# SBUF pools opened in another order, with pads, so that every float32r matmul operand starts at a multiple of 256 bytes

## The chip, the core and the metric

The kernel runs on one core of one Trainium2 chip. The metric is device time in microseconds (us) of one execution, the median of several runs. Engines are named as in the profile: PE (TensorE matmul), PEld (TensorE weight load), DVE (VectorE), ACT (ScalarE), POOL (GpSimd) and SP (SyncE, which issues the DMAs).

## The reference

A two-layer decoder trunk over 512 tokens of width 1024. Each layer is a half-step SwiGLU FFN, a token mixer and a second half-step FFN, each behind an RMS norm; a last norm ends it.

```python
def _swiglu(h, wg, wu, wd):                    # D_FF = 2816
    return (jax.nn.silu(h @ wg) * (h @ wu)) @ wd
...
    for i in range(DEPTH):                     # DEPTH = 2
        h = _rmsnorm(x, ffn1_norm[i])
        x = x + 0.5 * _swiglu(h, ffn1_w_gate[i], ffn1_w_up[i], ffn1_w_down[i])
        h = _rmsnorm(x, mix_norm[i])
        x = x + _mixing(h, positions, w_in[i], w_out[i], ...)
        h = _rmsnorm(x, ffn2_norm[i])
        x = x + 0.5 * _swiglu(h, ffn2_w_gate[i], ffn2_w_up[i], ffn2_w_down[i])
    return _rmsnorm(x, final_norm)
```

`_mixing` projects h through one matrix and runs three causal mixers on parts of the result: forgetting attention (4 heads of 64), dilated window attention (4 heads of 64, with rotary positions) and a gated linear recurrence (HGRN2, 4 heads of 128); their outputs go through one output matrix.

## The kernel before

The token dimension (512) lies along the free axis, the features in blocks of 128 on the partitions. Every large product is computed from two float32r halves of each operand: `load_split` loads a weight tile of up to 128x1024 float32 (`raw`, 3 buffers, a DMA on SP), ACT rounds it to float32r (`wh`, L243) and DVE takes the rest (`wl`, L245). Activations are split in the same way: `xh`, `xl` from x, `hh`, `hl` for the hidden layer, `oh..`, `ol..` for the mixers' outputs. `mm3` (L250 to L252) then issues three matmuls of 128x128 by 128x512 into the same PSUM tile:

```python
        PE.matmul(ps, lh, rh, start=first, stop=False)
        PE.matmul(ps, lh, rl, start=False, stop=False)
        PE.matmul(ps, ll, rh, start=False, stop=last)
```

The first operand is stationary (weights, loaded by PEld), the second is moving. Gate and up (tile `gu_ps`): 22 hidden blocks x 2 x 8 x 3 matmuls in each of 4 FFNs, weights from `wh`/`wl`, moving `xh`/`xl`. Down (`d_ps`): 8 x 22 x 3 in each FFN, moving `hh`/`hl`. The mixer's projections (`hf`, `hq`, `hi`, `dqk`, `v`, `hg`, `ff`, `fq`, `fk`) use `wh`/`wl` with `xh`/`xl` in either role (L425 to L427 are mm3 with the activations stationary). The output product (`o_ps`) has `oh`/`ol` moving. The matmuls within the mixers (`lv`, `ho`, `sc`, `po`, transposes) are plain float32.

A tile framework orders the instructions: it schedules the traced program for each engine by dependences and priorities (`high_priority(CHAIN)` for the mixers' chains), so projections fill PE between the chain's steps. Tiles with the same tag share a buffer, and a new user of a buffer waits for the old one.

SBUF tiles are placed one after another in the order in which pools are opened and their tiles are first made. In the built program the first pool begins 128 bytes past a multiple of 256. Tiles made by `lines` (statistics, scalars) are rounded up to 64 bytes; all others here but some tables are multiples of 256 bytes. Before, `const` comes first and starts with a 48-float `pad` (192 bytes); its tiles are 26 x 256 bytes in all. So `x`, `xh`, `xl`, `raw`, `wh`, `wl` begin 64 bytes past a multiple of 256. `small` shifts what follows by 128: `hh`, `hl`, and `oh`/`ol` in the mixer's pool, begin 192 bytes past. A 128-column slice is 512 bytes, so all slices used as operands keep these offsets.

In `states` (L680 to L688) four blocks b of two heads go through one PSUM tile (`ho_ps`, one buffer): up to four matmuls of a head, then DVE writes `ho` (L681), then ACT squares it into a scratch tile `hsq` and accumulates the sum in `hss` (L685). In `dilated`, DVE applies the rotary positions to `qk` through scratch tiles `ca` and `sa` (L592 to L598) before PE transposes it (`dt_ps`, L602). `hsq` and `ca` have 512 bytes and one buffer each.

Of the kernel before, what the change touches and what calls it, by code (L numbers as in the profile page):

```python
# [10 lines left out]
F32 = mybir.dt.float32  # L11
# [7 lines left out]
NB, KB, FB = T // 128, D // 128, FF // 128  # L19
# [6 lines left out]
LEVELS = (1, 2, 4, 8, 16, 32, 64)  # L26
AHEAD = 400
CHAIN = 100
PAD = 48


def shape_constants():
# [95 lines left out]
def hybrid_trunk(ctx: ExitStack, tc: tile.TileContext, a, out):  # L128
    nc = tc.nc
    V, S, G, PE = nc.vector, nc.scalar, nc.gpsimd, nc.tensor  # L130

    const = ctx.enter_context(tc.tile_pool(name="const", bufs=1))
    keep = ctx.enter_context(tc.tile_pool(name="keep", bufs=1))
    wp = ctx.enter_context(tc.tile_pool(name="wp", bufs=2))
    small = ctx.enter_context(tc.tile_pool(name="small", bufs=2))
    acc_p = ctx.enter_context(tc.tile_pool(name="acc", bufs=4, space=bass.MemoryType.PSUM))
    gen_p = ctx.enter_context(tc.tile_pool(name="gen", bufs=1, space=bass.MemoryType.PSUM))

    def lines(pool, shape, dt=F32, **kw):

        n = int(np.prod(shape[1:]))
        flat = pool.tile([shape[0], -(-n // 16) * 16], dt, **kw)[:, 0:n]
        if len(shape) == 2:
            return flat
        return flat.rearrange("p (a b) -> p a b", a=shape[1])
# [4 lines left out]
    def gen(tag, name):  # L150
        return gen_p.tile([128, 512], F32, tag=tag, name=name)


    const.tile([128, PAD], F32, name="pad")
    x = [keep.tile([128, T], F32, name=f"x{k}") for k in range(KB)]
    par = const.tile([128, 64], F32, name="par")
    raws = []
# [38 lines left out]
    def rsqrt(m, shape, tag):  # L196

        y = lines(small, shape, tag=tag + "y", name="rs_y")
        S.activation(y, m, AF.Sqrt)
        V.reciprocal(y, y)  # L200
        t = lines(small, shape, tag=tag + "t", name="rs_t")
        V.tensor_tensor(out=t, in0=y, in1=y, op=ALU.mult)
        V.tensor_tensor(out=t, in0=t, in1=m, op=ALU.mult)
        V.tensor_scalar(out=t, in0=t, scalar1=-0.5, scalar2=1.5, op0=ALU.mult, op1=ALU.add)
        r = lines(small, shape, tag=tag + "r", name="rs_r")
        V.tensor_tensor(out=r, in0=y, in1=t, op=ALU.mult)
        return r
# [190 lines left out]
    def mixing(l, after, r, rb):  # L398
# [7 lines left out]
        mp = ctx2.enter_context(tc.tile_pool(name="mix", bufs=1, reuse_waits="tile"))  # L406
# [23 lines left out]
        def slot(tag, shape, name, dt=F32, bufs=1):  # L430
            return mp.tile(list(shape), dt, tag=tag, name=name, bufs=bufs)
# [5 lines left out]
        otl = {kind: [pair(f"ol{kind}", f"ol{kind}", R32)] for kind in "fd"}  # L437
        amat, obl = {}, {}
        at = [lines(mp, [128, 8], tag=f"ad{p}", name=f"ad{p}") for p in range(2)]

        def put_out(kind, b, o, n):

            ps = gen("pt", "ot_ps")
            for i in range(n):
                PE.transpose(ps[:, i * 128:(i + 1) * 128], o[:, i * 128:(i + 1) * 128], ident)
            s = slice(b * 128, (b + 1) * 128)
            for i in range(n // 2):
                pv = ps[:, i * 256:(i + 1) * 256].rearrange("p (n t) -> p n t", n=2)
                hi, lo = oth[kind][i][:, :, s], otl[kind][i][:, :, s]
                S.copy(hi, pv)  # L450
                V.tensor_tensor(out=lo, in0=pv, in1=hi.bitcast(F32), op=ALU.subtract)
# [206 lines left out]
            return hv  # L658

        ho = [slot(f"ho{b}", (128, 4, 128), f"ho{b}") for b in range(NB)]  # L660
        hss = [lines(mp, [128, NB, 2], tag=f"hss{p}", name=f"hss{p}") for p in range(2)]
        hrs = [None, None]

        def states(p, hv):
            am, ob = amat[p], obl[p]
            for b in range(NB):
                po = gen("lv", "ho_ps")
                for hh in range(2):
                    cross = {
                        (0, 1): ob[:, 2, hh * 256:hh * 256 + 128],  # L670
                        (2, 3): ob[:, 2, hh * 256 + 128:hh * 256 + 256],
                        (0, 2): ob[:, hh, 0:128], (0, 3): ob[:, hh, 128:256],
                        (1, 2): ob[:, hh, 256:384], (1, 3): ob[:, hh, 384:512],
                    }
                    h = 2 * p + hh
                    hs = slice(h * 128, (h + 1) * 128)
                    ps = po[:, hh * 128:(hh + 1) * 128]
                    for j in range(b + 1):
                        lhs = cross[j, b] if j < b else am[:, hh, b * 128:(b + 1) * 128]
                        PE.matmul(ps, lhs, hv[j // 2][:, j % 2, hs], start=j == 0, stop=j == b)  # L680
                    V.scalar_tensor_tensor(out=ho[b][:, h, :], in0=hv[b // 2][:, b % 2, hs],  # L681
                                           scalar=at[p][:, hh * NB + b:hh * NB + b + 1], in1=ps,
                                           op0=ALU.mult, op1=ALU.add)
                    sq = mp.tile([128, 128], F32, tag="hsq", name="hsq", bufs=1)
                    S.activation(sq, ho[b][:, h, :], AF.Square, accum_out=hss[p][:, b, hh:hh + 1])  # L685
                yield
            ss = hss[p]
            V.tensor_scalar(out=ss, in0=ss, scalar1=1.0 / 128, scalar2=EPS, op0=ALU.mult, op1=ALU.add)  # L688
            hrs[p] = rsqrt(ss.rearrange("p b h -> p (b h)"), [128, 8], f"hr{p}")
# [20 lines left out]
        hv = values()  # L710
        run(d0)
        run(states(0, hv))
        run(decays(1, *decay_inputs(1)))
        run(states(1, hv))
        run(dilated())
        gated()
# [24 lines left out]
    for l in range(L):  # L741
        nrm = {}
        ffn(l, a["ffn1_w_gate"], a["ffn1_w_up"], a["ffn1_w_down"],
            lambda d: norm_block(d, gvec(("mix_norm", l), d), nrm), rb, None if l else tables)
        r, rb = norm_finish(nrm)
        nrm = {}
        with ExitStack() as ctx2:
            mixing(l, lambda d: norm_block(d, gvec(("ffn2_norm", l), d), nrm), r, rb)
        r, rb = norm_finish(nrm)
        nrm = {}  # L750
        if l + 1 < L:
            ffn(l, a["ffn2_w_gate"], a["ffn2_w_up"], a["ffn2_w_down"],
                lambda d: norm_block(d, gvec(("ffn1_norm", l + 1), d), nrm), rb)
            r, rb = norm_finish(nrm)
        else:
            def last(d):
                square_block(d, nrm)
                if d == KB - 2:
                    warm = lines(small, [128, 1], tag="warm", name="warm")
                    S.activation(warm, nrm["ss"][:, 0:1], AF.Sqrt)  # L760

            ffn(l, a["ffn2_w_gate"], a["ffn2_w_up"], a["ffn2_w_down"], last, rb)
            _, rb = norm_finish(nrm, copy=False)
            for d in range(KB):
                V.scalar_tensor_tensor(out=x[d], in0=x[d], scalar=gvec("final", d), in1=rb,
                                       op0=ALU.mult, op1=ALU.mult)
                (nc.scalar if d % 2 else nc.sync).dma_start(out=out[d * 128:(d + 1) * 128, :], in_=x[d])
# [17 lines left out]
```

## Time and profile before

| | |
|---|---|
| median of 3 runs | 2109.24 us (2109.0 to 2109.46) |
| profiled execution, its own time | 2108.85 us |
| its span, first to last instruction | 2107.1 us |
| mean granted TensorE clock | 0.997 |
| PE busy | 2080.3 us, 99% |
| DVE / ACT busy | 993.5 us (47%) / 691.6 us (33%) |
| DMA | 184.35 MB, mean 87 GB/s |

Matmuls overlap in the pipeline: a matmul's duration in the profile includes its drain, and its end is modelled. What a stream of matmuls costs is the distance from one start to the next.

### The profile page before, as it was taken

To read this page: it belongs to the slowest core of one execution; us is meant where nothing else is said; L and a number is where in the kernel's file an instruction comes from. 1 tells how busy PE (TensorE), PEld (TensorE's weight loads), DVE (VectorE), ACT (ScalarE), POOL (GpSimd) and SP (SyncE) were. 2 spreads that over 40 slices of the span, in tenths; PEclk is the share of its full clock that TensorE was granted. 3 is DMA by queue.
4 is the path that set the end of the run, shared out by engine and by line. 5 is a ranking of instruction groups with operands and counts; after the bars stand their busy time and mean duration, and the time that the engine had idled before them with its cause. 6 is when DMAs were issued, how large, how long until landed. Compare 5 with 4: busy or idle time off the path is not lost.

```text
span 2107.1 us, 23700 instructions
## 1 busy us (share of the span) xinstructions
PE 2080.3 (99%) x9622; PEld 1688.9 (80%) x9622; DVE 993.5 (47%) x1590; ACT 691.6 (33%) x1005; POOL 13.0 (1%) x18
## 2 busy tenths in 40 slices
PE   8999999999999999999999999999999999999997
PEld 6888888888777888888888888888887778888885
DVE  7444433556364544443344443336554554444323
ACT  5323222333353423222233322232344443323221
POOL 0000000000000000000000000000000000000000
PEclk9999999999999999999999999999999999999998
DMA  5322333211122222233332223332211122222332
GB/s 166 100 91 99 95 93 94 94 60 51 50 69 67 97 92 99 100 94 92 95 98 93 100 96 91 99 100 70 65 57 51 56 85 90 100 98 92 95 96 69
DMA packets 54373, 184.35 MB, mean 87 GB/s; under 512 B 6888, under 2 KB 7016, under 8 KB 54264
## 3 DMA queue, kind: packets, MB, share of 16 engines
q1 hardware_dynamic: 53656, 181.73, 27.1%
q8 instruction: 75, 1.23, 0.2%
q10 hardware_dynamic: 576, 1.05, 0.1%
q14 instruction: 34, 0.28, 0.0%
q0 software_dynamic: 32, 0.07, 0.0%
HBM read 180.69 MB, written 2.10 MB: 87 GB/s over the span
## 4 chain that ended last, share of the span: by engine, by line
PE 97%; DVE 2%; ACT 1%; DMA 0%; issue 0%; SPq 0%; DVEq 0%
PE gu_ps L252 15%; PE gu_ps L251 15%; PE gu_ps L250 15%; PE d_ps L252 8%; PE d_ps L250 8%; PE d_ps L251 8%; PE lv_ps L501 2%; PE sc_ps L552 2%; PE po L571 2%; PE o_ps L250 1%; PE o_ps L251 1%; PE o_ps L252 1%; PE ho_ps L680 1%; PE pt_ps L564 1%; PE v_ps L425 1%; PE v_ps L426 1%
## 5 line engine op out<-in xcount | busy, mean ns | idle before, releaser
L243 ACT CAST wh<-raw 128x1024 fp32r<-128x1024 f32 (+2 forms) x350 | 357.6, 1022 | 1112.7 <-issue 417.4
L245 DVE TENSOR_TENSOR wl<-raw,wh 128x1024 fp32r<-128x1024 f32 (+2 forms) x350 | 415.5, 1187 | 321.5 <-ACT wh L243 319.4
L250 PE MATMUL gu_ps<-xh,wh 128*128 128x512 f32 x1408 | 548.8, 390 | 7.5 <-ACT wh L243 7.5
L252 PE MATMUL gu_ps<-xh,wl 128*128 128x512 f32 x1408 | 550.4, 391 | 0.0
L251 PE MATMUL gu_ps<-xl,wh 128*128 128x512 f32 x1408 | 548.3, 390 | 0.0
L250 PEld LDWEIGHTS gu_ps<-xh,wh 128*128 128x128 f32 x1408 | 264.9, 188 | 63.6 <-ACT wh L243 7.5
L252 PEld LDWEIGHTS gu_ps<-xh,wl 128*128 128x128 f32 x1408 | 264.8, 188 | 56.1 <-issue 1.0
L251 PEld LDWEIGHTS gu_ps<-xl,wh 128*128 128x128 f32 x1408 | 264.8, 188 | 55.4 <-DVE xl L184 0.2
L252 PE MATMUL d_ps<-hh,wl 128*128 128x512 f32 x704 | 278.1, 395 | 0.0
L250 PE MATMUL d_ps<-hh,wh 128*128 128x512 f32 x704 | 278.1, 395 | 0.0
L251 PE MATMUL d_ps<-hl,wh 128*128 128x512 f32 x704 | 278.1, 395 | 0.0
L380 DVE TENSOR_TENSOR u<-gu_ps,rb 128x512 f32<-128x512 f32 x88 | 60.8, 691 | 269.2 <-PE gu_ps L252 269.0
L252 PEld LDWEIGHTS d_ps<-hh,wl 128*128 128x128 f32 x704 | 132.1, 188 | 32.2
L251 PEld LDWEIGHTS d_ps<-hl,wh 128*128 128x128 f32 x704 | 132.1, 188 | 32.1
L250 PEld LDWEIGHTS d_ps<-hh,wh 128*128 128x128 f32 x704 | 132.1, 188 | 32.1
L377 DVE TENSOR_TENSOR g<-gu_ps,rb 128x512 f32<-128x512 f32 x88 | 60.8, 691 | 178.7 <-PE gu_ps L252 176.6
L383 ACT CAST hh<-u 128x512 fp32r<-128x512 f32 x88 | 54.8, 623 | 61.2 <-DVE u L381 61.2
L394 DVE SCALAR_TENSOR_TENSOR x<-d_ps,x 128x512 f32<-128x512 f32 x32 | 22.1, 692 | 95.3 <-PE d_ps L252 95.3
L381 DVE TENSOR_TENSOR u<-u,g 128x512 f32<-128x512 f32 x88 | 60.9, 692 | 8.4
L501 PEld LDWEIGHTS lv_ps<-hQ,hk 128*128 128x128 f32 x448 | 55.8, 191 | 8.7 <-issue 5.9
L385 DVE TENSOR_TENSOR hl<-u,hh 128x512 fp32r<-128x512 f32 x88 | 60.3, 686 | 4.1 <-ACT hh L383 4.1
L571 PEld LDWEIGHTS po<-vv,pt 128*128 128x128 f32 x320 | 42.2, 190 | 19.7 <-DVE pt L569 7.8
(236 smaller groups left out, 2104.8 us busy)
## 6 DMA issues: line engine op xcount, KB each, us to landing
raw<-in_ffn_w_gate SPq DMA_DIRECT2D x88, 512.0 KB, 3.5
raw<-in_ffn_w_up SPq DMA_DIRECT2D x88, 512.0 KB, 3.5
raw<-in_w_in SPq DMA_DIRECT2D x58, 512.0 KB, 3.5
raw<-in_ffn_w_down SPq DMA_DIRECT2D x64, 448.0 KB, 3.3
raw<-in_ffn_w_down SPq DMA_DIRECT2D x32, 512.0 KB, 3.5
raw<-in_w_out_dh SPq DMA_DIRECT2D x16, 384.0 KB, 2.9
x<-in_x SPq DMA_DIRECT2D x8, 256.0 KB, 6.3
raw<-in_w_out_f SPq DMA_DIRECT2D x4, 512.0 KB, 3.6
```

Of the source, the lines that this page charges most:

```text
L243: S.copy(wh, raw)
L245: V.tensor_tensor(out=wl, in0=raw, in1=wh.bitcast(F32), op=ALU.subtract)
L250: PE.matmul(ps, lh, rh, start=first, stop=False)
L251: PE.matmul(ps, lh, rl, start=False, stop=False)
L252: PE.matmul(ps, ll, rh, start=False, stop=last)
L377: V.tensor_tensor(out=g, in0=part[0], in1=rb, op=ALU.mult)
L380: V.tensor_tensor(out=u, in0=part[1], in1=rb, op=ALU.mult)
L381: V.tensor_tensor(out=u, in0=u, in1=g, op=ALU.mult)
L383: S.copy(h1, u)
L385: V.tensor_tensor(out=h2, in0=u, in1=h1.bitcast(F32), op=ALU.subtract)
L501: PE.matmul(ps[:, e:e + 64], K[:, hh, s], Q[:, hh, s].rearrange("p (n two c) -> p n two c", two=2, c=c)[:, :, 1, :], start=True, stop=True)
L571: PE.matmul(po[:, h * HD:(h + 1) * HD], pt[:, j * 128:(j + 1) * 128], val[:, j, h * HD:(h + 1) * HD], start=j == 0, stop=j == b)
```

## The change

The `const` pool is opened after `keep` and `wp`; a 32-float tile (128 bytes) in a new first pool and a 96-float tile (384 bytes) in a new pool behind `small` are pads that nothing reads. The `hss` tiles are made earlier in the mixer's pool, and `hsq` takes the tag, and so the buffer, of `ca`. With it `x`, `xh`, `xl`, `raw`, `wh`, `wl`, `hh`, `hl` and all `oh`, `ol` begin at a multiple of 256 bytes. No instruction's shape or type changes.

```diff
-PAD = 48
+PAD = 96
...
-    const = ctx.enter_context(tc.tile_pool(name="const", bufs=1))
+
+    align = ctx.enter_context(tc.tile_pool(name="align", bufs=1))
     keep = ctx.enter_context(tc.tile_pool(name="keep", bufs=1))
     wp = ctx.enter_context(tc.tile_pool(name="wp", bufs=2))
+    const = ctx.enter_context(tc.tile_pool(name="const", bufs=1))
     small = ctx.enter_context(tc.tile_pool(name="small", bufs=2))
+    fill = ctx.enter_context(tc.tile_pool(name="fill", bufs=1))
...
-    const.tile([128, PAD], F32, name="pad")
+    align.tile([128, 32], F32, name="pad0")
+    fill.tile([128, PAD], F32, name="pad1")
     x = [keep.tile([128, T], F32, name=f"x{k}") for k in range(KB)]
...
         at = [lines(mp, [128, 8], tag=f"ad{p}", name=f"ad{p}") for p in range(2)]
+        hss = [lines(mp, [128, NB, 2], tag=f"hss{p}", name=f"hss{p}") for p in range(2)]
...
         ho = [slot(f"ho{b}", (128, 4, 128), f"ho{b}") for b in range(NB)]
-        hss = [lines(mp, [128, NB, 2], tag=f"hss{p}", name=f"hss{p}") for p in range(2)]
...
-                    sq = mp.tile([128, 128], F32, tag="hsq", name="hsq", bufs=1)
+                    sq = mp.tile([128, 128], F32, tag="ca", name="hsq", bufs=1)
```

The order of instructions is the same on SP and POOL. On PE, DVE and ACT it differs at one place in each layer, the second call of `states` (heads 2 and 3). On PE there, before (`v_ps` are matmuls of the value projection, `sc_ps`, `pt_ps` and `dt_ps` belong to the dilated attention):

```order
L680 MATMUL ho_ps<-hv_2813,ob_3384 128x128
L680 MATMUL ho_ps<-hv_2813,am_3288 128x128
L564 MATMUL pt_ps<-ident,neg 128x128
L552 MATMUL sc_ps<-dt_3464,dt_3463 128x128
L425 MATMUL v_ps_3649<-wh,xh_2167 128x512
L680 MATMUL ho_ps<-hv_2813,ob_3384 128x128 x2
L680 MATMUL ho_ps<-hv_2814,am_3288 128x128
L426 MATMUL v_ps_3649<-wl,xh_2167 128x512
L427 MATMUL v_ps_3649<-wh,xl_2169 128x512
L564 MATMUL pt_ps<-ident,neg 128x128
```

And on PE at the same place with the change (L684 was L680, L607 was L602, L429 was L425):

```order
L684 MATMUL ho_ps<-hv_2820,ob_3391 128x128 x2
L684 MATMUL ho_ps<-hv_2821,am_3295 128x128
L684 MATMUL ho_ps<-hv_2820,ob_3391 128x128 x2
L684 MATMUL ho_ps<-hv_2821,am_3295 128x128
L684 MATMUL ho_ps<-hv_2820,ob_3391 128x128 x2
L684 MATMUL ho_ps<-hv_2821,ob_3391 128x128
L684 MATMUL ho_ps<-hv_2821,am_3295 128x128
L684 MATMUL ho_ps<-hv_2820,ob_3391 128x128 x2
L684 MATMUL ho_ps<-hv_2821,ob_3391 128x128
L684 MATMUL ho_ps<-hv_2821,am_3295 128x128
L607 MATMUL dt_ps<-ident,qk 128x128 x4
L429 MATMUL v_ps_3658<-wh,xh_1989 128x512
```

All 20 `ho_ps` matmuls of the call now stand in a row, and the transposes of `qk` and the rest of the value projection follow them. On DVE with the change (L685 was L681, L597 to L603 were L592 to L598):

```order
L685 SCALAR_TENSOR_TENSOR ho_2684<-hv_2820,ad_2680,ho_ps 128x128 x2
L685 SCALAR_TENSOR_TENSOR ho_2685<-hv_2820,ad_2680,ho_ps 128x128 x2
L685 SCALAR_TENSOR_TENSOR ho_2686<-hv_2821,ad_2680,ho_ps 128x128 x2
L685 SCALAR_TENSOR_TENSOR ho_2687<-hv_2821,ad_2680,ho_ps 128x128 x2
L692 TENSOR_SCALAR hss_2682<-hss_2682 128x8
L597 TENSOR_TENSOR ca<-qk,rope 128x128
L603 TENSOR_TENSOR qk<-ca,sa 128x8x16
```

The first `ca` of `dilated` stood before these eight, among the work of `decays`; now it stands behind all of them, since it waits for the buffer that `hsq` uses.

## Rows read from the trace of the kernel before

**Rows 1.** The page: span, busy time by engine, PE in 40 slices.
```profile
span 2107.1 us, 23700 instructions
PE 2080.3 (99%) x9622; PEld 1688.9 (80%) x9622; DVE 993.5 (47%) x1590; ACT 691.6 (33%) x1005; POOL 13.0 (1%) x18
PE   8999999999999999999999999999999999999997
```

**Rows 2.** The page: the chain that ended last, by engine.
```profile
PE 97%; DVE 2%; ACT 1%; DMA 0%; issue 0%; SPq 0%; DVEq 0%
```

**Rows 3.** Groups by line and shape: count, busy us, mean ns, idle before.
```profile
L252 PE MATMUL gu_ps<-xh,wl 128*128 128x512 f32 x1408 | 550.4, 391 | 0.0
L252 PE MATMUL d_ps<-hh,wl 128*128 128x512 f32 x704 | 278.1, 395 | 0.0
L250 PEld LDWEIGHTS d_ps<-hh,wh 128*128 128x128 f32 x704 | 132.1, 188 | 32.1
L250 PE MATMUL hq_ps<-xh,wh 128*128 128x512 f32 x64 | 24.9, 390 | 0.0
L252 PE MATMUL o_ps<-ohf,wl 128*128 128x512 f32 x32 | 12.6, 395 | 0.0
```

**Rows 4.** Windows: a down stretch, a gate/up stretch; clock, DMA share, GB/s last.
```profile
267.00:372.00 105.00, 105.00 (x452) 84.46 (x451) 36.69 (x41) 29.29 (x35) 0.95 (x1) 1.00 0.32 95
700.00:950.00 250.00, 250.00 (x1102) 206.46 (x1101) 114.08 (x137) 75.49 (x93) 0.00 (x0) 1.00 0.29 96
```

**Rows 5.** Timeline, PE, gate/up: start us, us; first and last of 55 rows.
```profile
99.63 0.39 PE L251 MATMUL gu_ps<-xl,wh 128*128 128x512 f32 x1
99.86 0.39 PE L252 MATMUL gu_ps<-xh,wl 128*128 128x512 f32 x1
...
111.87 0.39 PE L251 MATMUL gu_ps<-xl,wh 128*128 128x512 f32 x1
```

**Rows 6.** Timeline, PE, down: first and last of 53 rows.
```profile
299.78 0.40 PE L252 MATMUL d_ps<-hh,wl 128*128 128x512 f32 x1
300.02 0.39 PE L250 MATMUL d_ps<-hh,wh 128*128 128x512 f32 x1
...
311.92 0.40 PE L250 MATMUL d_ps<-hh,wh 128*128 128x512 f32 x1
```

**Rows 7.** Timeline, PE, output product: first and last of 49 rows.
```profile
660.73 0.39 PE L250 MATMUL o_ps<-ohf,wh 128*128 128x512 f32 x1
...
671.89 0.39 PE L252 MATMUL o_ps<-ohB,wl 128*128 128x512 f32 x1
```

**Rows 8.** Timeline around 606 and 2090: matmuls with no weight load beside them.
```profile
605.93 0.39 PE L250 MATMUL fq_ps<-xh,wh 128*128 128x512 f32 x1
607.13 0.30 PEld L552 LDWEIGHTS sc_ps<-fka,fqa 66*128 66x128 f32 x2 [1.24 <-DVE fka L648]
2090.22 0.40 PE L252 MATMUL d_ps<-hh,wl 128*128 128x512 f32 x1
2092.84 0.30 PEld L213 LDWEIGHTS ss_ps<-ones,ss 128*128 128x128 f32 x2 [2.67 <-issue]
```

**Rows 9.** Groups by line, and timeline, of `states` and the rotary step.
```profile
L681 DVE SCALAR_TENSOR_TENSOR ho<-hv,ad,ho_ps 128x128 f32<-128x128 f32 x32 | 11.1, 346 | 18.5 <-PE ho_ps L680 18.3
L680 PEld LDWEIGHTS ho_ps<-hv,ob 128*128 128x128 f32 x96 | 13.0, 190 | 3.5 <-DVE ho L681 2.5 <-issue 0.7
L680 PE MATMUL ho_ps<-hv,ob 128*128 128x128 f32 x96 | 15.0, 278 | 0.0
L685 ACT ACTIVATE hsq<-ho 128x128 f32<-128x128 f32 x32 | 9.8, 307 | 19.3 <-DVE ho L681 18.1 <-DVE den L574 1.2
L685 ACT ACTIVATION_READ_ACCUMULATOR hsq<-ho 128x1 f32 x32 | 6.0, 187 | 0.0
510.53 0.29 DVE L592 TENSOR_TENSOR ca<-qk,rope 128x128 f32<-128x128 f32 x1
511.22 0.29 DVE L598 TENSOR_TENSOR qk<-ca,sa 128x128 f32<-128x128 f32 x1
```

## Prediction

> **What bounds the kernel now.** I read the page first: PE is busy for 99% of the span, in all 40 slices [rows 1], and the chain that ended last is 97% PE [rows 2]. DVE and ACT have half and two thirds of their time free. So the time is the sum of what PE's instructions cost one after another, and a change helps as far as it shortens their spacing or hurts as far as it opens a gap between them.
>
> Next I read what the PE time consists of. The groups by line and shape [rows 3] have their counts: three gate/up groups of 1408, three down groups of 704, and for the mixers 18 projection groups of 64, six of 32 and three of 16 (the `hq` row is one of the first kind), and output products in three groups of 64 and six of 32 (the `ohf` row is one of the second). That is 4224 + 2112 + 1392 + 384 = 8112 float32r matmuls of 512 columns. Their mean durations of 390 to 395 ns contain the drain, so I took spacing from the timeline: in gate/up 55 rows lie between 99.63 and 111.87, 12.24 us over 54 steps, 226.7 ns [rows 5]; in down 53 rows from 299.78 to 311.92, 12.14 over 52, 233.5 ns [rows 6]; in the output product 49 rows from 660.73 to 671.89, 11.16 over 48, 232.5 ns [rows 7]. Long windows say the same, taking off the two matmuls that reach over their edges: 105 us / 450 = 233.3 ns and 250 / 1100 = 227.3 [rows 4].
>
> [...] The two streams have the same shapes; what differs between them is the start of the moving operand, 64 bytes past a multiple of 256 in gate/up and the projections, 192 past in down and the output product, while the stationary operand is at 64 in all of them (for the projections, both are). A loss that differs by the place of an operand and not by its shape is the first ground for the change. [...]
>
> [...] The next weights are loaded (188 ns, [rows 3]) while a matmul runs, and could take reads from it. [...]
>
> **The change, part by part.** *Alignment.* All operands start at 0 past 256. If the whole excess is due to the start, spacing falls to the 213.3 ns that the columns take: gate/up 4224 x 13.4 ns = 56.5 us; down 2112 x 20.2 = 42.6; projections 1392 x 13.4 = 18.6, taken at the gate/up spacing because their offsets and their mean (390 ns, [rows 3]) are the same; output 384 x 19.2 = 7.4. Together 125 us. The lower bound is 0 (nothing depends on the start). [...]
>
> Do the others keep up? In gate/up 24 matmuls pass per weight tile, 5.4 us now and 5.1 then. DVE is busy 46% and ACT 30% of that window, DMA 29% at 96 GB/s [rows 4]; 6% more pace leaves them far from their limits. That cover is why I add nothing here.
>
> *The shared buffer of `hsq` and `ca`.* Nothing is added, but order changes. `ca` now waits for the squares of the second `states` call, so the rotary step, the transposes and the fillers that depend on `dqk_ps` buffers stand behind it, and PE has 20 `ho_ps` matmuls in a row with nothing between. Each of the 8 heads-and-blocks needs the PSUM tile back: DVE's 346 ns after the last matmul, then a weight load of 190 ns [rows 9], 0.54 us in which PE has nothing; before, projections filled it, and the matmuls themselves waited little (2.5 us in all, at the weight loads, [rows 9]). Seven handoffs and the one that leads out, in two layers: 16 x 0.54 = 8.6 us. Behind them `dt_ps` waits for the last square (307 + 187 ns) and for `ca` and `qk` (0.29 each, [rows 9]): 1.07 us, twice: 2.1. Together 10.8, taken as 11. Lower bound 5 (if half of each handoff overlaps the drain of the matmul, which is 278 ns long [rows 9]), upper 17 (if each costs 0.8 with the drain, and the table load and squares delay `dt_ps` further). The displaced projections run later and cost the same.
>
> *Fillers get shorter.* In the mixers the projections hide chains of DVE and ACT work. The 1776 matmuls there save 18.6 + 7.4 = 26 us; where the chain is longer than its filler the gain is lost again. PE shows hardly an idle moment now, so most fits; I take a quarter as lost, 6 us (bounds 0 and 13).
>
> *Pads, pool order, `hss`.* No instruction; the order on SP and POOL is unchanged. 0.
>
> Sum: 125 - 11 - 6 = 108 us. Against the profiled execution's own 2108.85 us that gives 2000.9; the median of the runs is 0.4 above it, so 2001.
>
> **The rivals.** *The offset between the operands counts, not the start.* [...] Then the change, which puts all at 0, only brings down and output to 226.7: 2112 x 6.8 + 384 x 5.8 = 16.6 us, less 11 for the order: 2103.5. [...]
>
> *The start counts for nothing (the other side).* The excess is what a float32r matmul costs, larger in down because of where its stream settles. [...] Then only the handoffs of `states` remain: 2109 + 11 = 2120, up to 2126. It decides if alignment saves under 11 us, 1.4 ns per matmul. [...] Against: gate/up and down have one shape and two spacings.
>
> *Part of the excess only.* If a third of the 125 us came, 42 - 12 = 30 us, 2079; this lies between the first two and takes no chance of its own beyond their edges.
>
> **How the numbers follow.** Chances: alignment saves most of the excess 0.58, the offset between operands 0.16, nothing 0.26. The predicted time is that of the first, 2001. Its own range: down to 1985 if neither handoffs nor fillers cost (2108.9 - 125 = 1984), up to 2025 if 2.4 ns remain per matmul (19 us) with 5 us more lost in the mixers. The range of 8 in 10 has to reach over the offset rival and begin the third: 1985 to 2118, which leaves out most of that one (2114 to 2126) and little else. About 0.2%, 4 us, is what a measurement of this kernel can tell from no change. Faster by more than that: the first case and over half of the second (2103.5 is 0.27% below), 0.67. Within: the rest of the second and the third where the handoffs cost least, 0.09. Slower: 0.24.
>
> **What would show it.** Right: timeline spacing of `gu_ps` and `d_ps` alike at 213 to 216 ns, durations near 0.375; the window that holds 1100 gate/up matmuls shrinks from 250 to some 236 us; PE idle grows by about 11 us at the second `states` call, as waits of `ho_ps` on DVE `ho`; DVE, ACT and DMA busy times unchanged. Offset rival: `gu_ps` stays at 226.7 and only `d_ps` falls to it. Third: both stay. I would also be wrong if a faster PE ran into its weights, seen as `gu_ps` waiting for ACT `wh` all along the FFNs, or if the handoffs cost several times 0.54 us.

## The result and the profile after

The change makes the kernel slower: 2121.93 us (median of 4 runs, 2119.03 to 2123.3) against 2109.12 (2108.46 to 2109.46), a ratio of 1.0059, 95% interval 1.0042 to 1.0077. The profiled execution took 2121.13 us of its own time, with a span of 2119.4. I had forecast 2001.

The page after: span, busy times, and PE and the clock that it was granted in 40 slices.

```profile
span 2119.4 us, 23702 instructions
PE 2081.7 (98%) x9622; PEld 1699.2 (80%) x9622; DVE 993.0 (47%) x1590; ACT 690.2 (33%) x1003; POOL 12.9 (1%) x18
PE   8999999998999999999999999999989999999997
PEclk9999999998999999999999999999989999999998
```

Compare with [rows 1]: PE's row had no digit below 9 between its ends, and now has two 8s, one in each layer. The clock has an 8 in the same two slices.

Groups by line and shape (busy us, mean ns of one, idle before), then the timeline of PE in gate/up and in down, first and last of 55 rows each.

```profile
L256 PE MATMUL gu_ps<-xh,wl 128*128 128x512 f32 x1408 | 550.6, 391 | 0.0
L256 PE MATMUL d_ps<-hh,wl 128*128 128x512 f32 x704 | 274.0, 389 | 0.0
...
99.54 0.39 PE L256 MATMUL gu_ps<-xh,wl 128*128 128x512 f32 x1
...
111.78 0.39 PE L256 MATMUL gu_ps<-xh,wl 128*128 128x512 f32 x1
...
299.46 0.39 PE L256 MATMUL d_ps<-hh,wl 128*128 128x512 f32 x1
...
311.70 0.39 PE L256 MATMUL d_ps<-hh,wl 128*128 128x512 f32 x1
```

Both streams now take 12.24 us over 54 steps, 226.7 ns. Gate/up is where it was [rows 5], with the group's mean at 391 ns as before [rows 3]; down came from 233.5 [rows 6] to the gate/up spacing, and its mean from 395 ns to 389. That is the alignment's whole effect in the FFNs: by these stretches 2112 x 6.8 = 14.4 us saved, and not a nanosecond in gate/up.

Where more than that was lost stands in the waits of PE (us in total, times, longest):

```profile
PE ho_ps L684 <- DVE ho L685: 6.2, 14, 0.4
PE dt_ps L607 <- DVE qk L603: 3.3, 2, 1.7
PE v_ps L429 <- ACT qk L594: 1.6, 2, 0.8
PE ho_ps L684 <- ACT ob L542: 1.1, 2, 0.5
```

These are 12.2 us, all at the second call of `states` and the rotary step behind it. The timeline of PE there, in the first layer:

```profile
508.98 0.49 PE L684 MATMUL ho_ps<-hv,am 128*128 128x128 f32 x2 [0.44 <-DVE ho L685]
509.91 0.49 PE L684 MATMUL ho_ps<-hv,ob 128*128 128x128 f32 x2 [0.44 <-DVE ho L685]
510.23 0.39 PE L684 MATMUL ho_ps<-hv,am 128*128 128x128 f32 x2
...
511.65 0.63 PE L684 MATMUL ho_ps<-hv,am 128*128 128x128 f32 x2
512.72 1.22 PE L684 MATMUL ho_ps<-hv,ob 128*128 128x128 f32 x4 [0.44 <-DVE ho L685]
...
522.97 0.66 PE L607 MATMUL dt_ps<-ident,qk 128*128 128x128 f32 x4 [1.66 <-DVE qk L603]
524.41 0.79 PE L429 MATMUL v_ps<-wh,xh 128*128 128x512 f32 x1 [0.78 <-ACT qk L594]
```

Besides the gaps in brackets the reader should look at the same pair of `ho_ps<-hv,am` matmuls: 0.39 us at 510.23 and 0.63 at 511.65. The windows say why (stretch; its length, then busy time of PE, PEld, DVE, ACT and POOL; PEclk; DMA share; GB/s):

```profile
500.00:530.00 30.00, 23.96 (x99) 18.55 (x97) 10.73 (x44) 9.57 (x26) 0.00 (x0) 0.74 0.05 18
507.00:510.50 3.50, 2.08 (x11) 1.24 (x9) 0.69 (x2) 1.39 (x5) 0.00 (x0) 1.00 0.00 0
510.50:521.00 10.50, 8.31 (x33) 7.01 (x32) 1.73 (x5) 2.01 (x10) 0.00 (x0) 0.51 0.00 2
521.00:524.40 3.40, 0.97 (x7) 0.55 (x5) 2.42 (x11) 2.54 (x5) 0.00 (x0) 1.00 0.00 0
524.40:531.30 6.90, 6.89 (x20) 4.97 (x21) 3.94 (x21) 2.61 (x5) 0.00 (x0) 0.51 0.00 0
1558.60:1565.50 6.90, 5.58 (x24) 4.70 (x22) 1.04 (x3) 1.33 (x8) 0.00 (x0) 0.51 0.00 0
1568.90:1575.80 6.90, 6.01 (x20) 4.39 (x20) 4.25 (x23) 3.99 (x7) 0.00 (x0) 0.51 0.00 0
```

In four stretches the granted clock is 0.51. PE is busy there for 8.31 + 6.89 + 5.58 + 6.01 = 26.8 us; by the two clocks, 0.51 and 1.00, I estimate that outside such a stretch it would have been at least half of that, so up to 13.4 us lost (the pair above took 0.39 us instead of 0.63). The same 30 us of the kernel before had a clock of 1.00 and PE busy for all but 0.1:

```profile
500.00:530.00 30.00, 29.90 (x167) 23.53 (x166) 18.73 (x67) 16.74 (x42) 0.00 (x0) 1.00 0.11 36
```

So the account is: about 16 us saved in down and output (14.4 and, by the prediction's 5.8 ns for each of 384, 2.2), 12 lost to gaps, up to 13 to the clock, a net loss of 9 to 10 where 12.8 was measured; some 3 us stay unaccounted for. That the second and third belong to the shared buffer, and what is left in the 226.7 ns, the experiments had to show.

### The profile page after: what moved, and what is told of

Read it like the earlier page. It is cut to its first block, busy times and chain, and to the rows that moved or that the text cites. A ratio compares the mean times of both kernels' runs of the same rounds, so it can differ in the third digit from the quotient of the medians.

```text
span 2119.4 us, 23702 instructions
## 1 busy us (share of the span) xinstructions
PE 2081.7 (98%) x9622; PEld 1699.2 (80%) x9622; DVE 993.0 (47%) x1590; ACT 690.2 (33%) x1003; POOL 12.9 (1%) x18
## 3 DMA queue, kind: packets, MB, share of 16 engines
q1 hardware_dynamic: 53656, 181.73, 26.8%
## 4 chain that ended last, share of the span: by engine, by line
PE 96%; DVE 2%; ACT 1%; issue 0%; DMA 0%; SPq 0%; DVEq 0%; ACTq 0%
PE gu_ps L254 15%; PE gu_ps L256 15%; PE gu_ps L255 15%; PE d_ps L255 8%; PE d_ps L256 8%; PE d_ps L254 8%; PE lv_ps L506 2%; PE sc_ps L557 2%; PE po L576 2%; PE o_ps L254 1%; PE o_ps L255 1%; PE o_ps L256 1%; PE ho_ps L684 1%; PE pt_ps L569 1%; PE v_ps L429 1%; PE v_ps L430 1%
```

## The experiments

My theory after the result: the distance between the two operands' starts costs, not the start; and sharing `hsq` with `ca` costs idle time and, by it, clock. Rivals: the start of the moving operand alone counts; the slow place comes with the new addresses rather than with the sharing; the clock falls for some other reason than the gaps.

**1. The change without the sharing.**

```diff
-                    sq = mp.tile([128, 128], F32, tag="ca", name="hsq", bufs=1)
+                    sq = mp.tile([128, 128], F32, tag="hsq", name="hsq", bufs=1)
```

> The change with one line undone: hsq has its own buffer again, all starts stay at 0 past 256. If the shared buffer costs the time (the gaps at the second states call and the 1.2 GHz stretches behind them) and the down and output products keep their 226.7 ns: 2109 - 17 = 2092 to 2094 us, granted clock 1.00 from 500 to 530 us, no waits of ho_ps on DVE ho over 1 us in all. Rival (the pads or the pool order cost it): it stays at 2115 to 2122 us.

Measured: 2094.59 us (2093.63 to 2094.92), ratio to before 0.9932, 0.9918 to 0.9947. The page, and the window at the place of the loss:

```profile
span 2092.8 us, 23700 instructions
PE 2066.6 (99%) x9622; PEld 1689.5 (81%) x9622; DVE 993.6 (47%) x1590; ACT 692.2 (33%) x1005; POOL 13.0 (1%) x18
...
500.00:530.00 30.00, 29.91 (x159) 23.38 (x159) 16.39 (x57) 15.01 (x40) 0.00 (x0) 1.00 0.16 49
```

No wait of `ho_ps` on DVE is left, the clock stays at 1.00, and both spacings are 226.7 ns. The alignment alone is worth 14.5 us (2109.12 - 2094.59; 14.1 against the kernel before as it was timed beside this run, 2108.67); the sharing cost 27.3 on top of it (2121.93 - 2094.59). This version beats both kernels.

**2. The sharing without the alignment**, in the kernel before:

```diff
-                    sq = mp.tile([128, 128], F32, tag="hsq", name="hsq", bufs=1)
+                    sq = mp.tile([128, 128], F32, tag="ca", name="hsq", bufs=1)
```

> The kernel before with only hsq in the buffer of ca; starts stay at 64 and 192. If the shared buffer alone costs 28 us: 2136 to 2139 us, ho_ps waits of some 6 us, 1.2 GHz stretches at both second states calls, d_ps at 233 ns. Rival (the cost needs the new placement): 2109 us.

Measured: 2137.95 us (2130.8 to 2140.32), ratio 1.0142, 1.0126 to 1.0159; down at 233.3 ns. The sharing costs 29 us here (its four executions spread over 9.5), where it cost 27 above, so the new addresses are not needed for it. The windows of its profiled execution:

```profile
511.00:523.60 12.60, 7.31 (x45) 5.40 (x44) 3.72 (x13) 4.83 (x18) 0.00 (x0) 1.00 0.00 1
523.60:530.60 7.00, 6.22 (x21) 4.16 (x19) 4.29 (x24) 3.62 (x7) 0.00 (x0) 0.51 0.01 2
1562.00:1574.90 12.90, 7.58 (x46) 5.48 (x44) 4.12 (x15) 5.25 (x20) 0.00 (x0) 1.00 0.00 0
1574.90:1581.90 7.00, 6.27 (x18) 4.47 (x18) 4.37 (x22) 3.15 (x6) 0.00 (x0) 0.51 0.00 0
```

The waits of PE are those of the change to the tenth (`ho_ps` on `ho` 6.2 us, `dt_ps` 3.3, `v_ps` 1.6), but each layer has one stretch at 0.51, not two, and it begins behind the wait for `qk`. This execution, of 2130.8 us, is the shortest of the four, with a mean clock of 0.994; the others have 0.988 to 0.990 and took 2136 to 2140. In these four the longer times go with the lower clocks; only this execution has a profile, so that the other three have the same gaps is likely and not shown.

**3. All operands at 128 past a multiple of 256**, `hsq` with its own buffer:

```diff
-    align.tile([128, 32], F32, name="pad0")
+    align.tile([128, 64], F32, name="pad0")
```

> As e1, with pads that put every float32r operand at 128 past a multiple of 256 instead of 0. If only the offset between stationary and moving counts (0 in both): 226.7 ns in all streams, the same time as e1, 2092 to 2094. If multiples of 256 count: gate/up or down at 230 ns or more, 2105 us or more.

Measured: 2093.78 us, ratio 0.9929, 0.9915 to 0.9944, and 226.7 ns in both streams. The timelines of gate/up and of down, first and last of 54 rows each:

```profile
99.78 0.39 PE L255 MATMUL gu_ps<-xl,wh 128*128 128x512 f32 x1
...
111.79 0.39 PE L254 MATMUL gu_ps<-xh,wh 128*128 128x512 f32 x1
...
298.79 0.39 PE L254 MATMUL d_ps<-hh,wh 128*128 128x512 f32 x1
...
310.81 0.39 PE L256 MATMUL d_ps<-hh,wl 128*128 128x512 f32 x1
```

12.01 and 12.02 us over 53 steps. Both starts at 128 gave the 226.7 ns that experiment 1 has with both at 0: here the starts did not have to be multiples of 256 bytes, only alike.

**4. Only the weights' halves moved, by 128**, with `xh`, `hh`, `oh` and their partners left at 0:

```diff
-PAD = 96
+PAD = 64
...
+    gap = ctx.enter_context(tc.tile_pool(name="gap", bufs=1))
     wp = ctx.enter_context(tc.tile_pool(name="wp", bufs=2))
...
+    gap.tile([128, 32], F32, name="pad2")
```

> As e1, with a pad between the pools of the activations and of the weights: wh and wl at 128 past a multiple of 256, xh, xl, hh, hl, oh, ol at 0. If the offset between the two operands counts, gate/up and projections now lose as down did before, all 8112 matmuls at 232 to 233.5 ns: e1 + 8112 x 6.5 ns = 53 us, 2145 to 2150. If only the moving operand's own start counts (it stays at 0): 2092 to 2094, as e1.

Measured: 2133.07 us, ratio 1.0119, 1.0104 to 1.0134. The timeline in gate/up, first and last of 53 rows:

```profile
99.75 0.39 PE L258 MATMUL gu_ps<-xh,wl 128*128 128x512 f32 x1
...
111.83 0.39 PE L256 MATMUL gu_ps<-xh,wh 128*128 128x512 f32 x1
```

12.08 us over 52 steps, 232.3 ns, in a stream whose moving operand begins at a multiple of 256. The theory that only the moving start counts is refuted. Against experiment 1 it costs 38.5 us: gate/up 4224 x 5.6 = 24, down (232.5 ns) 2112 x 5.8 = 12, the rest in the mixers. I had expected 53, with the projections and the output product paying as much for each matmul as these two; together their 1776 matmuls added some 2 us. What moved here, of the operands of gate/up, is only the weights, which the weight loads read; the moving reads stand where they stood in experiment 1.

**5. Sharing, with two PSUM tiles for `states`:**

```diff
-                po = gen("lv", "ho_ps")
+                po = gen(("lv", "sc")[b % 2], "ho_ps")
```

> The changed kernel with hsq still in the buffer of ca, but the four blocks of states alternate between two PSUM tiles (lv and sc), so a block's matmuls need not wait for DVE's ho of the block before. In the order, 9 to 11 ho_ps matmuls stand before the transposes of qk where 20 stood. My theory: the price of sharing is the idle time of PE at the handoffs and, behind them, the stretches at clock 0.5; with most ho_ps gaps gone the ho_ps waits fall from about 6 us to under 2, no clock row of 0.5 follows them, and only the dt_ps wait (3.3 us in two) stays: 2096 to 2101 us. Rival: the price is the chain through the shared buffer (last square, ca, qk, dt_ps) and what stands behind it, whatever the ho_ps matmuls do: the clock rows of 0.5 stay and the time stays at 2115 to 2122.

Measured: 2107.0 us (2106.41 to 2108.42), ratio 0.9992, 0.9983 to 1.0001: neither theory's number. The waits of PE, and the windows:

```profile
PE dt_ps L607 <- DVE qk L603: 5.1, 2, 2.5
PE v_ps L429 <- ACT qk L594: 1.6, 2, 0.8
PE ho_ps L684 <- DVE ho L685: 1.3, 4, 0.4
...
509.00:514.50 5.50, 3.29 (x24) 2.72 (x23) 1.65 (x5) 3.12 (x15) 0.00 (x0) 1.00 0.01 3
514.50:521.40 6.90, 5.14 (x15) 3.66 (x16) 4.85 (x25) 4.69 (x9) 0.00 (x0) 0.51 0.01 2
1555.60:1562.50 6.90, 6.63 (x19) 4.79 (x20) 4.13 (x23) 2.68 (x5) 0.00 (x0) 0.51 0.00 0
```

The `ho_ps` waits fell as expected, but `dt_ps` now arrives early and waits 2.5 us each time, and the clock still falls once in each layer, during that wait. 8 us of gaps and, for the clock, up to half of 5.14 + 6.63 make 13.9; the span is 12.9 above that of experiment 1. So more than half of the price goes with the handoffs (and with the row of 20, which is broken up here too), and the chain through the shared buffer has a part of its own.

**6. Operands 32 and 64 bytes apart**, `hsq` with its own buffer:

```diff
-PAD = 96
+PAD = 112
...
+    gap = ctx.enter_context(tc.tile_pool(name="gap", bufs=1))
     wp = ctx.enter_context(tc.tile_pool(name="wp", bufs=2))
...
+    gap.tile([128, 8], F32, name="pad2")
```

> hsq with its own buffer; an 8-float tile before wp and a longer pad behind small put the weights' halves 32 bytes past a multiple of 256 with the moving xh, xl at 0, and hh, hl, oh, ol at 96, so that the two operands of gate/up are 32 bytes apart and those of down and output 64. What is open: whether any distance that is no multiple of 256 costs, or 128 alone. Any distance costs alike: gu and d at about 232.5 ns, 2094.6 + 38.5 = 2133 us. Only 128 costs: both stay at 226.7, 2094 to 2095. The cost grows with the distance (5.7 ns at 128, so 1.4 at 32 and 2.9 at 64): gu about 228, d about 229.6, 4224 x 1.4 + 2112 x 2.9 and a little for output and projections, 2107 to 2110.

Measured: 2131.37 us, ratio 1.0107, 1.0093 to 1.0121. Gate/up (53 rows) and down (54 rows):

```profile
99.81 0.40 PE L256 MATMUL gu_ps<-xh,wh 128*128 128x512 f32 x1
...
111.94 0.40 PE L257 MATMUL gu_ps<-xl,wh 128*128 128x512 f32 x1
...
298.75 0.39 PE L257 MATMUL d_ps<-hl,wh 128*128 128x512 f32 x1
...
310.88 0.39 PE L256 MATMUL d_ps<-hh,wh 128*128 128x512 f32 x1
```

12.13 / 52 = 233.3 ns at 32 bytes, 12.13 / 53 = 228.9 at 64. But the four down stretches of this run, one in each FFN, are not alike. Windows within the first and the third:

```profile
260.00:375.00 115.00, 115.00 (x504) 94.33 (x504) 39.45 (x45) 31.85 (x38) 0.95 (x1) 1.00 0.33 98
1312.00:1427.00 115.00, 115.00 (x494) 93.17 (x493) 38.74 (x43) 30.28 (x38) 0.41 (x1) 1.00 0.33 97
```

Taking off the two matmuls at the edges, 115 us / 502 = 229.1 ns and 115 / 492 = 233.7; the second and the fourth hold 504, as the first does. The tiles, their starts and the shapes are the same in all four, so at 64 bytes the distance alone does not settle the spacing: it took either of two values. Every distance tried that is no multiple of 256 costs something, 32 as much as 128, and 64 less in three stretches of four. "128 alone" and "grows with the distance" are both refuted; "all alike" fits the total within 2 us but not those three. The two distances also lie in opposite directions (at 32 the stationary operand starts further on, at 64 the moving one), and each was tried in its own streams: 32 in gate/up and the projections, 64 in down and output.

**7. All halves in bfloat16** in place of float32r:

```diff
-R32 = mybir.dt.float32r
+R32 = mybir.dt.bfloat16
```

What is open is to what the 226.7 ns belong, which a 512-column matmul took at every start tried with its two operands alike.

> hsq with its own buffer, and all halves (xh, xl, wh, wl, hh, hl, the outputs' halves) in bfloat16 instead of float32r, so with less of the operands' precision; shapes and the number of matmuls as before, weight loads as instructions of their own. [...] They belong to operands of four bytes: gu spacing 213 to 216 ns, and with all 8112 matmuls 11 to 13.4 ns shorter 1986 to 2006 us. They belong to every 512-column matmul of this stream: 226.7 ns, 2090 to 2095 us.

Measured: 2009.11 us (2007.82 to 2009.74), ratio 0.9527, 0.9514 to 0.954. Gate/up, first and last of 48 rows:

```profile
33.22 0.38 PE L257 MATMUL gu_ps<-xh,wl 128*128 128x512 bf16 x1
...
43.36 0.38 PE L256 MATMUL gu_ps<-xl,wh 128*128 128x512 bf16 x1
```

10.14 / 47 = 215.7 ns: 11.0 ns of the 226.7 go with the type. 8112 x 11.0 = 89 us; 2094.6 - 89 = 2005.4, and the run took 2009.1. The type changes the weight loads as well:

```profile
L256 PEld LDWEIGHTS <-wh 128*128 128x128 bf16 x2448 | 240.3, 98 | 281.4 <-issue 0.6
```

One takes 98 ns, where a float32r one takes 188 [rows 3]. So the run does not tell whether the 11 ns belong to the matmul's own read or to the longer weight load beside it.

**8. Sharing, with the gaps filled:**

```diff
+                    if p and done:
+                        fill_ps = gen("sc", "fill_ps")
+                        n = 6 if len(done) == 7 else 1
+                        for _ in range(n):
+                            PE.matmul(fill_ps[:, 0:256], done[-1], ob[:, 0, 0:256],
+                                      start=True, stop=True)
+                    done.append(ho[b][:, h, :])
```

> The changed kernel, hsq in the buffer of ca as there, with matmuls that nothing reads put into the gaps: in the second call of states one plain float32 matmul of 256 columns (a finished ho block by ob, into the PSUM tile of sc) behind each head's ho_ps matmuls and six behind the last, so that PE works while it waits for DVE's ho and for qk. In the order they stand between the ho_ps groups and ahead of the transposes of qk. My theory: the clock fell to 0.5 because PE stood idle again and again there, so with the gaps filled no row of 0.5 is left at that place, and the sharing costs only the time of the gaps (12.1 us in the two layers) and what the fillers run over: 2106 to 2110 us. Rival: the clock falls for another reason at this place (the float32 matmuls of 128 columns themselves, or the row of 20 of them): the rows of 0.5 stay, 2119 to 2125.

Measured: 2111.69 us (2110.9 to 2113.47), ratio 1.0014, 1.0005 to 1.0023. The windows around the place, in both layers:

```profile
508.00:523.00 15.00, 13.21 (x73) 9.56 (x72) 6.12 (x25) 5.98 (x20) 0.00 (x0) 1.00 0.01 2
1549.50:1564.50 15.00, 13.21 (x73) 9.53 (x72) 6.11 (x25) 5.98 (x20) 0.00 (x0) 1.00 0.00 1
```

The 20 `ho_ps` matmuls, the chain through the shared buffer and the order are still there, and the clock is 1.00 throughout. Useless work made the kernel 10 us faster than the change, although it overruns the gaps (its span is 17.4 us above that of experiment 1, where the gaps of the change had been 12.2, and its time 2 us above my range). The rival is refuted: the clock, 0.51 at this place in the change, fell because PE stood idle.

## Why the prediction was wrong, point by point

- **What bounds the kernel:** right. PE's spacing, its gaps and its clock account for every run above to about 4 us.
- **"If the whole excess is due to the start, spacing falls to the 213.3 ns":** this is the step that failed, and some 110 of its 125 us with it: 14.5 came. No run shows the 213.3 ns, nor the 2.4 ns of the range: the shortest spacings that I read were 226.7 ns with float32r halves and 215.7 with bfloat16 ones, so the excess over 213.3 was not measured. I chose the upper end, all of it due to the start. The kernel before (gate/up, at 64) and experiments 1 (at 0) and 3 (at 128) show 226.7 ns at three different starts, and experiment 7 that 11.0 ns of them come with the float32r halves. Why they cost that much is not shown. A sign was there: a bound of 0 that I had kept only in the range.
- **The rival of the offset between operands:** this is what happened to the alignment, to its own sign (gate/up unmoved, only down falls to it) and nearly to its size: 16.6 us worked out, 14.5 measured in experiment 1. I gave it 0.16, since it leaves gate/up at 226.7 ns; but it did not have to explain those, as they can have a cause of their own (11.0 ns of them go with the type, experiment 7). The rival with the nearest time (2120, "nothing") was near by accident: it had no gain and a cost of 11, where there were a gain of 14.5 and a cost of 27.
- **The shared buffer, 11 us:** place and mechanism were right, and the idle time as well (12.2 us against 10.8: the 14 handoffs 0.44 each where I had 0.54, the wait for `qk` 1.66 where I had 1.07, and 0.78 for `v_ps` and 0.54 for `ob`, which I had left out). The missing term is the clock: up to 13.4 us by the windows, at least the 10 that experiment 8 gave back. The profile gives it as a share of full speed, 0.51 in these stretches; the frequency by which the expectations of experiments 1 and 2 call them is shown by no run. I had written that I would be wrong if the handoffs cost several times 0.54; the buffer cost two and a half times my 11 us (27.3), above my upper bound of 17, and not by the handoffs' length.
- **Shorter fillers, 6 us:** not tested, since the projections were no shorter.
- **The weight load beside a matmul:** I named it as something that could take reads from the running matmul, and gave it no part in the sum. Matmuls that had none beside them lasted 0.39 and 0.40 us [rows 8], as the others do, but ends are modelled, and experiment 4 speaks against leaving the weight load out: only what the weight loads read was moved, and gate/up went from 226.7 to 232.3 ns. For the 11 ns of the type it stays open (experiment 7).

Left open: why 64 bytes cost less than 32 or 128 in three stretches and as much in the fourth; the mechanism behind the distance at all; whether the 11 ns of the type are the matmul's or the weight load's; and which gaps bring the clock down. In the first layer of experiment 2 eight gaps passed at 1.00 and the clock fell behind the ninth, in the change it fell at the fourth. In experiment 2 the waits and the clock also leave about 3 of the profiled execution's 22 us unexplained.

## What to carry to other kernels

Look at the distance between the starts of a matmul's two operands: here the gate/up and down streams of float32r matmuls ran 2 to 7 ns slower for each wherever it was no multiple of 256 bytes (32, 64 and 128 were tried), and where pads brought it to 0 they took 226.7 ns (experiments 1 and 3). When two streams differ, only the difference speaks for what differs between them; the part that both have needs a test of its own, for instance with another type. And before two chains share a scratch buffer, to make room for pads too, look at what the new wait takes away from PE's fillers, and price a row of gaps on PE at about twice its idle time (27 us for 12 here, 12 for 8 in experiment 5), since here the clock fell to 0.51 behind it.

## What the runs showed of the hardware that was not expected

- A float32r matmul of 512 columns takes 226.7 ns from start to start, a bfloat16 one 215.7, in stretches of gate/up with no wait (the granted clock 1.00 in the windows of [rows 4], 0.9 or more in the slice of experiment 7's page that holds its rows).
- Distance of the operands' starts, modulo 256 bytes, and spacing in gate/up or down: 0, 226.7 ns (with starts at 0, 64 and 128); 32, 233.3; 64, 228.9 in three stretches and 233.7 in one; 128, 232.3 to 233.5.
- The place of the weights alone changed it: 226.7 to 232.3 ns in gate/up with the moving operands where they were (experiments 1 and 4).
- At rows of gaps of up to 2.5 us between groups of matmuls (4 gaps, 4 us in a layer, in experiment 5; 10 gaps, 6 us, in the change) the granted clock fell from 1.00 to 0.51 for 7 to 10 us at a time. With all but 1.8 us a layer of them filled (experiment 8) it stayed at 1.00.
